# One 129-column product for the high and low values of three query blocks in four, and one bfloat16 product for a tile's sum of squares

## The chip, the cores and the metric

The kernel runs on one core of a Trainium2 chip. The core has a matrix engine (PE, with weight loads listed apart as PEld), three engines for elementwise work (DVE, ACT, POOL), a queue engine (SP) and 16 DMA engines. Each compute engine works through its own instructions in order. The metric is the device time of one execution in microseconds (us); lower is better.

## The reference, cut to what matters

One decoder layer over 2048 tokens of width 1024: a normalised and modulated input, one input projection, two attention branches (A, forgetting attention over all earlier keys; B, sliding window), a gate on each, an output projection, a second normalisation and the residual. The change lies in the value product of branch A and in a scale of the output projection.

```
def forgetting_attention(q, k, v, f_logit):
    cum = jnp.cumsum(jax.nn.log_sigmoid(f_logit), axis=1)
    ...
        s = jnp.einsum('bhqd,bhkd->bhqk', qb, kh) * scale
        s = s + cb[..., None] - cum[:, :, None, :]
        s = jnp.where(causal, s, -jnp.inf)
        p = jax.nn.softmax(s, axis=-1)
        return jnp.einsum('bhqk,bhkd->bhqd', p, vh)
...
y = jnp.concatenate([oa, ob], axis=-1) @ w_out[l]
x = x + gate[:, None, :] * rms_norm(y, g_post[l])
```

Branch A has 8 heads of 64 columns. Inputs and output are float32.

## The kernel before

Products of float32 accuracy are made from 16-bit parts: a value is split into a high part (float16) and a low part (what is left, again in float16), and a product is the sum of high by high, high by low and low by high. For a value block of head `hd` and key block `b` the tile `vt[:, b, hd, :]` holds 129 columns (`VW = 129`): columns 0 to 63 the high part, column 64 ones, columns 65 to 128 the low part. The column of ones gives the sum of the softmax weights in the same product.

The program runs in three stages that overlap at their ends: projections and branch B (until about 420 us), branch A (until about 1000 us), and the output projection (from about 950 us to the end). In all of them the order of the work is written out by hand.

**Branch A.** A head is cut into 4 chunks of 512 queries (`ci` 0 to 3), and a chunk into steps of two key blocks: 2, 4, 6 and 8 steps, 20 for a head and 160 in all. A chunk's four 128-query blocks are numbered `u` 0 to 3. A step goes through these stations:

- `scores` (lines 1341 to 1352): the products into the PSUM tile `sta`;
- `exp32` (1356, ACT): the exponential into `p`, three buffers;
- `high` (1360, ACT) and `low` (1363, DVE): the high and the low part of the weights into `pha`, three buffers;
- `pv` (1365 to 1377, PE), two steps later: for each key block and each query block at or below the diagonal three products, high by high with the ones (65 columns, line 1373), high by low (64 columns, 1375) and low by high with the ones (65 columns, 1376), each with a weight load of its own, all added into columns 0 to 64 of block `u` of the PSUM tile `poa`.

After the last step of a chunk (lines 1378 to 1383) DVE takes the reciprocal of the sums (`a_ri`) and multiplies the four blocks by it in one instruction, out of PSUM into `ona`. `poa` has one buffer. So the first value product of the next chunk (line 1373) waits until DVE has read the last of `poa`.

The main loop issues for each step: its `exp32`, the `low` of the step before, a half of the other work (projections for the next heads, line 351; products for a row maximum, line 1300, whose DVE reductions are lines 1303 and 1305; on DVE also weight maxima, splits and gates), its `high`, the next step's `scores`, the `pv` of two steps before, and the other half. The row-maximum products, projections and small products share five PSUM banks named `bk`.

**Output projection.** For each of the 16 tiles of 128 tokens, `Out.turn` makes the gated input, sums its squares on ACT into one column `gs` (line 1510), adds that column over the 128 partitions with a product of a matrix of ones (line 1514, float32, one column wide), and derives a scale from the bits of the sum (`root_scale`, lines 125 to 129: a rough reciprocal square root by a shift, undone later by `inv`). The tile is split with that scale (1524 and 1525) and multiplied by the output weights (line 1576).

Of the kernel before, what the change touches and what calls it, by code (L numbers as in the profile page):

```python
# [10 lines left out]
F32 = mybir.dt.float32  # L11
F16 = mybir.dt.float16
BF16 = mybir.dt.bfloat16
# [3 lines left out]
ALU = mybir.AluOpType  # L17
AX = mybir.AxisListType

P = 128  # L20
# [4 lines left out]
CH = 512  # L25
# [10 lines left out]
XM, XR, VW = 66, 69, 129  # L36
# [7 lines left out]
def hybrid_layer(  # L44
# [17 lines left out]
    V, A, G, PE, SP = nc.vector, nc.scalar, nc.gpsimd, nc.tensor, nc.sync  # L62
# [20 lines left out]
    def sm(n, tag):  # L83
        return small.tile([P, n], F32, tag=tag, name=tag)
# [40 lines left out]
    def root_scale(dst, ss):  # L125

        h = small.tile([P, 1], I32, tag="rs_h", name="sc_h")
        V.tensor_scalar(h[:], ss.bitcast(I32), 1, None, op0=ALU.logical_shift_right)
        V.tensor_scalar(dst.bitcast(I32), h[:], -1, 0x5F3759DF + (15 << 23), op0=ALU.mult, op1=ALU.add)
# [35 lines left out]
    ones = const.tile([P, P], F32, name="ones")  # L165
# [20 lines left out]
    def bank(hold=False):  # L186
        n = next(n for n in order_ if n not in held)
        order_.remove(n)
        order_.append(n)
        if hold:  # L190
            held.add(n)
        return n
# [9 lines left out]
    def after(n, f):  # L202
        late.append([n, f])
# [79 lines left out]
    def o_store(on, pool, ci, rows_, cols_, eng, lag):  # L283
        if ci == 0:
            eng.dma_start(o_d[0][rows_, cols_].rearrange("(u p) c -> p u c", p=P), on)
            return
        u0, u1 = rows_.start // P, rows_.stop // P
        oh = pool.tile([P, u1 - u0, 2, on.shape[-1]], F16, tag="oh", name="oh")

        def low():  # L290
            V.tensor_tensor(oh[:, :, 1], on, oh[:, :, 0], op=ALU.subtract)
            eng.dma_start(o_d[ci][u0:u1, :, :, cols_].rearrange("u n p c -> p (u n) c"),
                          oh[:].rearrange("p u n c -> p (u n) c"))

        after(lag, lambda: A.activation(oh[:, :, 0], on, AF.Copy))
        after(lag + 1, low)
# [134 lines left out]
    def turn(ci, k, px=None):  # L431

        px = px or ps_x.tile([P, CH], F32, tag="x", name="px")
        for u in range(4):
            PE.transpose(px[:, u * P:(u + 1) * P], xt[ci * 4 + u][:, k * P:(k + 1) * P], ident[:])
        hf = hst.tile([P, CH], F32, tag="hf", name="hf")
        hi, lo = hT[ci][:, 0, k, :], hT[ci][:, 1, k, :]

        def scaled():
            for dst in ([hi] if k % 2 == 0 else []) + [hf[:]]:  # L440
                A.activation(dst, px[:], AF.Identity, scale=Gp[:, k:k + 1], bias=Shp[:, k:k + 1])

        def split():
            if k % 2:
                V.tensor_copy(hi, hf[:])
            V.tensor_tensor(lo, hf[:], hi, op=ALU.subtract)

        return scaled, split

    def turn_x(ci, k):  # L450
        scaled, split = turn(ci, k)
        after(1, scaled)
        after(2, split)
# [9 lines left out]
    start = ExitStack()  # L463
    st = start.enter_context(tc.tile_pool(name="start", bufs=1, reuse_waits="tile"))
    wad = start.enter_context(tc.tile_pool(name="wad", bufs=8, reuse_waits="tile"))
    with tc.manual_schedule():
# [172 lines left out]
        w_low("kb", 0, 1)  # L639
        w_low("vb", 0, 1)  # L640
        turned = [turn(0, k) for k in range(5)]
        squares(1)
        shf0 = col8("shf0")
# [9 lines left out]

        PE.transpose(bk[0][0:1, 0:P], bmx[:], ident[:])
        turned += [turn(0, k, bk[k - 4]) for k in (5, 6)]
        bm = st.tile([1, 1], F32, name="bm")
        V.tensor_reduce(bm[:], bk[0][0:1, 0:P], axis=AX.X, op=ALU.max)
# [215 lines left out]
    class Pair:  # L873
# [65 lines left out]
        def pv(self):  # L939
            j, i = self.j, self.i  # L940
            po = ps_pv.tile([P, 4, 64], F32, tag="pv", name="pob")
            for e, (i_, k0, nk) in enumerate(self.blocks):
                for h in range(2):
                    for b in range(nk):
                        for n, (pp_, vv) in enumerate(((0, 0), (0, 1), (1, 0))):
                            PE.matmul(po[:, 2 * e + h, :], self.ptt[b + 2 - nk][:, pp_, 2 * e + h, :],
                                      vb[:, k0 + b, self.g, 64 * vv:64 * vv + 64],
                                      start=(b == 0 and n == 0), stop=(b == nk - 1 and n == 2))

            def out_():  # L950
                on = onp.tile([P, 2, P], F32, tag="on", name="on")
                V.tensor_tensor(on[:].rearrange("p e (h d) -> p (e h) d", h=2), po[:],
                                self.rinv[:].unsqueeze(2).broadcast_to([P, 4, 64]), op=ALU.mult)
                o_store(on[:], onp, i // 4, slice((i % 4) * P, (i % 4 + 2) * P), slice((4 + j) * P, (5 + j) * P), G, 1)

            after(1, out_)
# [248 lines left out]
    def fox_pool(name, bufs, **kw):  # L1205
        return fox.enter_context(tc.tile_pool(name=name, bufs=bufs, reuse_waits="tile", **kw))

    ps_st = fox_pool("ps_st", 1, space=PSUM)
    ps_po = fox_pool("ps_po", 1, space=PSUM)
# [57 lines left out]
    vt, lk, lq = fx["vt"], fx["lk"], fx["lq"]  # L1267
# [63 lines left out]
    class Step:  # L1331
# [33 lines left out]
        def pv(self):  # L1365
            hd, ph = self.hd, self.ph
            if self.first:
                self.po_[0] = ps_po.tile([P, 4, 65], F32, tag="po", name="poa")
            po = self.po_[0]
            for n, (b, u0, o) in enumerate(self.blocks):  # L1370
                for u in range(u0, 4):
                    pq = slice(o + (u - u0) * P, o + (u - u0 + 1) * P)
                    PE.matmul(po[:, u, :], ph[:, 0, pq], vt[:, b, hd, 0:65],  # L1373
                              start=(self.first and n == 0 and u == 0), stop=False)
                    PE.matmul(po[:, u, 0:64], ph[:, 0, pq], vt[:, b, hd, 65:VW], start=False, stop=False)  # L1375
                    PE.matmul(po[:, u, :], ph[:, 1, pq], vt[:, b, hd, 0:65], start=False,  # L1376
                              stop=(self.last and n == len(self.blocks) - 1))
            if self.last:
                rinv = sm(4, "a_ri")
                V.reciprocal(rinv[:], po[:, :, 64])  # L1380
                on = op_.tile([P, 4, 64], F32, tag="ona", name="ona")
                V.tensor_tensor(on[:], po[:, :, 0:64], rinv[:].unsqueeze(2).broadcast_to([P, 4, 64]), op=ALU.mult)  # L1382
                o_store(on[:], op_, self.ci, slice(0, CH), slice(hd * 64, (hd + 1) * 64), SP, 1 if hd == 7 else 2)

        po_ = {}
# [76 lines left out]
    class Out:  # L1462
# [24 lines left out]
        def turn(self, lag):  # L1487

            if self.t < 4:
                px = [bk[bank()][:].rearrange("p (k n) -> p k n", k=4) for _ in range(2)]  # L1490
                for k in range(KT):
                    PE.transpose(px[k // 4][:, k % 4, :], self.o[:, k * P:(k + 1) * P], ident[:])
            self.hl = wpool.tile([P, 2, KT, P], F16, tag=("whl", "wraw")[self.t % 2], name="oz")
            self.sc = sm(1, "w_pw")
            hi, lo = self.hl[:, 0], self.hl[:, 1]
            gs = sm(1, "w_mx")

            def gate():
                if self.t < 4:
                    for h in range(2):  # L1500
                        z = self.z[:, 4 * h:4 * h + 4, :]
                        V.tensor_tensor(z, px[h], z, op=ALU.mult)
                    return
                of = ozp.tile([P, KT, P], F32, tag="of", name="of")
                V.tensor_tensor(of[:], self.oT[:, 0], self.oT[:, 1], op=ALU.add)
                V.tensor_tensor(self.z, of[:], self.z, op=ALU.mult)  # L1506

            def squares_():
                junk = stp.tile([P, KT, P], BF16, tag="st", name="zj")
                A.activation(junk[:], self.z, AF.Square, accum_out=gs[:])  # L1510

            def scale_():
                pg = bk[bank()][:, 0:1]
                PE.matmul(pg, ones[:], gs[:], start=True, stop=True)  # L1514
                root_scale(self.sc[:], pg)

                self.inv = sm(1, "w_sw")
                V.tensor_tensor(self.inv[:], self.sc[:], ysc[:], op=ALU.mult)
                V.reciprocal(self.inv[:], self.inv[:])

            after(1, gate)
            after(2, squares_)
            after(lag, scale_)
            after(lag + 1, lambda: A.activation(hi, self.z, AF.Copy, scale=self.sc[:]))
            after(lag + 2, lambda: V.scalar_tensor_tensor(lo, self.z, self.sc[:], hi, op0=ALU.mult, op1=ALU.subtract))  # L1525
# [109 lines left out]
    with tc.manual_schedule():  # L1635
# [35 lines left out]
        for s, stp_ in enumerate(steps):  # L1671
            hd, r = divmod(s, NS)
# [111 lines left out]
```

## Time and profile before

| | us |
|---|---|
| time, median of 3 runs | 1157.41 (1156.38 to 1158.7) |
| the profiled execution | 1157.8 |
| its span, from the first to the last instruction | 1156.1 |
| PE busy | 1116.8 (97% of the span) |
| DVE busy | 930.5 (80%) |
| ACT busy | 661.4 (57%) |

The groups of instructions name a line, an engine, an operation, the tiles written and read, a shape and a count, then the busy time in us, the mean of one in ns, and the idle time before them. A matmul's row runs from its start until its results are out, and the next one starts long before that; so how long a stream of products takes is read from the distances of their starts. In the timeline the first number is the start from the beginning of the span, the second how long the instruction, or the merged run of instructions, lasted. A bracket behind a row tells how long the engine was idle before it and what ended that.

### The profile page before, as it was taken

What the parts mean: (1) busy time and instruction counts of PE and PEld (TensorE: products, weight loads), DVE (VectorE), ACT (ScalarE), POOL (GpSimd) and SP (SyncE); (2) the same over time, 40 slices, a digit from 0 to 9 for tenths busy, and PEclk for the clock granted to TensorE, in tenths of its full rate; (3) what the DMA queues carried; (4) which work ended last, traced back from release to release, by engine and by line L of the source; (5) the groups of instructions that cost most, each with busy time, mean ns of one, the idle gap of its engine ahead of it and who ended that gap; (6) DMA issues with size and microseconds to landing.
All of it is one profiled execution on the core that took longest, in us unless ns stands there. A gap on an engine that the chain in (4) does not pass through costs nothing. (4 is left out here: it accounts for less than half of the span.)

```text
span 1156.1 us, 25291 instructions
## 1 busy us (share of the span) xinstructions
PE 1116.8 (97%) x9869; PEld 656.3 (57%) x9869; DVE 930.5 (80%) x2137; ACT 661.4 (57%) x1150; POOL 207.5 (18%) x332
## 2 busy tenths in 40 slices
PE   5899999999999999999999999999999999999997
PEld 2475544577765866555555555555555555544444
DVE  7877468987888568788988899888888887878885
ACT  2876344654555421666757666666776778534332
POOL 1122134554556530010010110001000000000000
PEclk9899999999999999999999999999999999999999
DMA  9943355433243232442344342123311337686743
GB/s 333 336 116 72 87 78 96 97 63 90 52 92 88 58 87 58 73 108 29 80 64 87 84 67 70 38 49 76 45 43 34 91 101 206 140 225 197 199 135 109
DMA packets 123476, 120.10 MB, mean 104 GB/s; under 512 B 64948, under 2 KB 100828, under 8 KB 123356
## 3 DMA queue, kind: packets, MB, share of 16 engines
q1 hardware_dynamic: 112088, 85.69, 27.6%
q0 software_dynamic: 10832, 32.50, 13.5%
q8 instruction: 77, 1.26, 0.6%
q14 instruction: 43, 0.35, 0.1%
q10 hardware_dynamic: 436, 0.28, 0.1%
HBM read 64.75 MB, written 25.18 MB: 78 GB/s over the span
## 5 line engine op out<-in xcount | busy, mean ns | idle before, releaser
L1356 ACT ACTIVATE p<-sta,lift,scl_qk 128x1024 f32<-128x1024 f32 (+2 forms) x160 | 172.0, 1075 | 131.6 <-PE sta L1350 82.6
L351 PE MATMUL bk<-hT,wh_qk 128*128 128x512 f16 x768 | 194.7, 378 | 0.0
L1363 DVE TENSOR_TENSOR pha<-p,pha 128x1024 f16<-128x1024 f32 (+2 forms) x160 | 169.1, 1057 | 0.2 <-ACT pha L1360 0.2
L1303 DVE TENSOR_REDUCE a_m<-bk 128x1 f32<-128x512 f32 x192 | 130.4, 686 | 45.8 <-PE bk L1300 44.8
L1576 PE MATMUL bk<-wohl,oz 128*128 128x512 f16 x744 | 165.3, 379 | 1.1 <-DVE oz L1525 0.7
L1360 ACT ACTIVATE pha<-p 128x1024 f16<-128x1024 f32 (+2 forms) x160 | 148.1, 926 | 5.9 <-PE poa L1376 1.2
L1576 PEld LDWEIGHTS <-oz 128*128 128x128 f16 x744 | 71.9, 99 | 82.8 <-DVE oz L1525 1.8
L1376 PE MATMUL poa<-vt,pha 128*128 128x65 f16 x1088 | 116.1, 192 | 1.4 <-DVE pha L1363 1.2
L1373 PE MATMUL poa<-vt,pha 128*128 128x65 f16 x1088 | 116.6, 193 | 0.8 <-DVE ona L1382 0.7
L1375 PE MATMUL poa<-vt,pha 128*128 128x64 f16 x1088 | 116.6, 194 | 0.0
L351 PEld LDWEIGHTS <-wh_qk 128*128 128x128 f16 x768 | 72.1, 97 | 74.4 <-issue 2.1
L1349 PE MATMUL sta<-T 128*128 128x512 f16 (+1 forms) x320 | 110.9, 346 | 2.8 <-ACT p L1356 2.7
L1300 PE MATMUL bk<-T 66*128 66x512 f16 (+2 forms) x320 | 109.7, 348 | 2.4 <-DVE a_m L1303 1.9
L1373 PEld LDWEIGHTS <-pha 128*128 128x128 f16 x1088 | 101.5, 96 | 15.5 <-DVE ona L1382 1.9
L1350 PE MATMUL sta<-T 69*128 69x512 f16 (+1 forms) x320 | 109.8, 348 | 0.0
L1375 PEld LDWEIGHTS <-pha 128*128 128x128 f16 x1088 | 100.9, 97 | 11.4
L1376 PEld LDWEIGHTS <-pha 128*128 128x128 f16 x1088 | 100.8, 99 | 1.8 <-DVE pha L1363 1.7
L351 PE MATMUL bk<-hT,wh_za 128*128 128x512 f16 x384 | 99.7, 378 | 0.0
L369 PE MATMUL bk<-wh_va,hT 128*128 128x256 f16 x768 | 91.9, 273 | 0.0
L351 PE MATMUL bk<-hT,wh_zb 128*128 128x512 f16 x384 | 91.6, 379 | 0.2 <-DVE qc L754 0.2
L351 PE MATMUL bk<-hT,wh_qb 128*128 128x512 f16 x384 | 91.2, 379 | 0.0
L369 PEld LDWEIGHTS <-hT 128*128 128x128 f16 x768 | 73.3, 98 | 12.2 <-issue 2.1
(459 smaller groups left out, 1919.7 us busy)
## 6 DMA issues: line engine op xcount, KB each, us to landing
hT<-in_x_dram SPq DMA_DIRECT2D x20, 512.0 KB
wa<-in_w_ada_dram SPq DMA_DIRECT2D x16, 512.0 KB
z_d<-tz POOLq DMA_DIRECT2D x32, 256.0 KB, 3.0
T<-z_d SPq DMA_DIRECT2D x16, 512.0 KB
T<-stq SPq DMA_DIRECT2D x62, 128.0 KB
out_dram<-hT SPq DMA_DIRECT2D x15, 512.0 KB
xt<-in_x_dram SPq DMA_DIRECT2D x12, 512.0 KB
qs<-qf SPq DMA_DIRECT2D x80, 64.0 KB
```

What stands on the lines that cost most here:

```text
L351: PE.matmul(ps, whl[:, a, k, :], hT[ci][:, b, k, :], start=(k == 0 and n == 0), stop=(k == KT - 1 and n == 2))
L369: PE.matmul(ps[:, (u % 2) * 2 * P:(u % 2 + 1) * 2 * P], hT[ci][:, a, k, u * P:(u + 1) * P], wv[p][:, b, k, :], start=(k == 0 and n == 0), ...
L1303: V.tensor_reduce(m3[:, u, pc:pc + 1], mx[:, :w], axis=AX.X, op=ALU.max)
L1349: PE.matmul(self.st[:, o:o + w], T[:, 3, kb_], T[:, 1, qc], start=True, stop=False)
L1350: PE.matmul(self.st[:, o:o + w], T[0:XR, 2, kb_], T[0:XR, 0, qc], start=False, stop=not diag)
L1356: A.activation(self.p32[:, :self.w], self.st[:, :self.w], AF.Exp, scale=scl[f"qk{self.hd}"][:], bias=lift[:])
L1360: A.activation(self.ph[:, 0, :self.w], self.p32[:, :self.w], AF.Copy)
L1363: V.tensor_tensor(self.ph[:, 1, :self.w], self.p32[:, :self.w], self.ph[:, 0, :self.w], op=ALU.subtract)
L1373: PE.matmul(po[:, u, :], ph[:, 0, pq], vt[:, b, hd, 0:65], start=(self.first and n == 0 and u == 0), stop=False)
L1375: PE.matmul(po[:, u, 0:64], ph[:, 0, pq], vt[:, b, hd, 65:VW], start=False, stop=False)
L1376: PE.matmul(po[:, u, :], ph[:, 1, pq], vt[:, b, hd, 0:65], start=False, stop=(self.last and n == len(self.blocks) - 1))
L1576: PE.matmul(py, self.hl[:, i, k, :], w_slot(8 * j + k)[:, cc], start=(k == 0 and m_ == 0), stop=(k == KT - 1 and m_ == 2))
```

## The change

Two places are edited. In `Step.pv` the products high by high and high by low become one product of 129 columns for query blocks 0, 1 and 2, whose results lie side by side in PSUM (block `u` begins at column 129 `u`). Four such blocks would be 516 columns, and the tile is one bank of 512; so block 3 keeps the three products and its 65 columns. The normalisation has to add the two halves of blocks 0 to 2. In `Out.turn` the column of sums of squares enters its product as bfloat16, read as the upper 16 bits of each float32, and so does the matrix of ones; the scale that comes of it may differ by a little, and is undone by the same `inv`.

```
-                self.po_[0] = ps_po.tile([P, 4, 65], F32, tag="po", name="poa")
-            po = self.po_[0]
+                self.po_[0] = ps_po.tile([P, CH], F32, tag="po", name="poa")
+            whole = self.po_[0]
+            po = [whole[:, VW * u:VW * u + (VW if u < 3 else 65)] for u in range(4)]
...
-                    PE.matmul(po[:, u, :], ph[:, 0, pq], vt[:, b, hd, 0:65],
+                    PE.matmul(po[u], ph[:, 0, pq], vt[:, b, hd, 0:VW if u < 3 else 65],
                               start=(self.first and n == 0 and u == 0), stop=False)
-                    PE.matmul(po[:, u, 0:64], ph[:, 0, pq], vt[:, b, hd, 65:VW], start=False, stop=False)
-                    PE.matmul(po[:, u, :], ph[:, 1, pq], vt[:, b, hd, 0:65], start=False,
+                    if u == 3:
+                        PE.matmul(po[u][:, 0:64], ph[:, 0, pq], vt[:, b, hd, 65:VW], start=False, stop=False)
+                    PE.matmul(po[u][:, 0:65], ph[:, 1, pq], vt[:, b, hd, 0:65], start=False,
                               stop=(self.last and n == len(self.blocks) - 1))
...
-                V.reciprocal(rinv[:], po[:, :, 64])
+                V.reciprocal(rinv[:], whole[:, 64:3 * VW + 65:VW])
                 on = op_.tile([P, 4, 64], F32, tag="ona", name="ona")
-                V.tensor_tensor(on[:], po[:, :, 0:64], rinv[:].unsqueeze(2).broadcast_to([P, 4, 64]), op=ALU.mult)
+                p3 = whole[:, 0:3 * VW].rearrange("p (u c) -> p u c", u=3)
+                V.tensor_copy(on[:, 0:3], p3[:, :, 65:VW])
+                V.tensor_tensor(on[:, 0:3], p3[:, :, 0:64], on[:, 0:3], op=ALU.add)
+                V.tensor_scalar(on[:, 3], po[3][:, 0:64], rinv[:, 3:4], None, op0=ALU.mult)
+                V.tensor_tensor(on[:, 0:3], on[:, 0:3], rinv[:, 0:3].unsqueeze(2).broadcast_to([P, 3, 64]), op=ALU.mult)
...
             gs = sm(1, "w_mx")
+            gs1 = gs[:].bitcast(BF16)[:, 1:2]
...
-                PE.matmul(pg, ones[:], gs[:], start=True, stop=True)
+                PE.matmul(pg, ones[:].bitcast(BF16).rearrange("p (n two) -> p two n", two=2)[:, 1], gs1,
+                          start=True, stop=True)
```

Of the 1088 triples of value products 768 belong to blocks 0 to 2 (in a head, block `u` meets 4 `ci` + `u` + 1 key blocks in chunk `ci`: 28, 32 and 36 over the four chunks, 96, times 8 heads), and 320 to block 3.

Three places show what the change moves. The first is PE in `pv`, in the first step of the program that has all four query blocks. `pha` are the weights' high and low parts. Before, each query block is:

```order
L1373 LDWEIGHTS pha
L1373 MATMUL poa<-vt,pha 128x65
L1375 LDWEIGHTS pha
L1375 MATMUL poa<-vt,pha 128x64
L1376 LDWEIGHTS pha
L1376 MATMUL poa<-vt,pha 128x65
```

Now, for blocks 2 and 3 (the shapes name the columns of the product):

```order
L1374 LDWEIGHTS pha
L1374 MATMUL poa<-vt,pha 128x129
L1378 LDWEIGHTS pha
L1378 MATMUL poa<-vt,pha 128x65
L1374 LDWEIGHTS pha
L1374 MATMUL poa<-vt,pha 128x65
L1377 LDWEIGHTS pha
L1377 MATMUL poa<-vt,pha 128x64
L1378 LDWEIGHTS pha
L1378 MATMUL poa<-vt,pha 128x65
```

Block 2 has lost a product and its weight load; block 3 stands as before.

The second is DVE at the end of the first head. Before:

```order
L1303 TENSOR_REDUCE a_m<-bk_138 128x1
L1380 RECIPROCAL a_ri<-poa 128x4
L1382 TENSOR_TENSOR ona<-poa,a_ri 128x256
L1303 TENSOR_REDUCE a_m<-bk_6030 128x1
L1363 TENSOR_TENSOR pha<-p_7565,pha 128x384
```

Now:

```order
L1382 RECIPROCAL a_ri<-poa 128x4
L1385 COPY ona<-poa 128x192
L1386 TENSOR_TENSOR ona<-poa,ona 128x192
L1387 TENSOR_SCALAR ona<-poa,a_ri 128x64
L1388 TENSOR_TENSOR ona<-ona,a_ri 128x192
L1303 TENSOR_REDUCE a_m<-bk_6030 128x1
L1363 TENSOR_TENSOR pha<-p_7479,pha 128x384
```

One instruction became four, three of which read `poa`; the reduction and the split behind them keep their order.

The third is PE around the sum of squares in the output projection (`oz` is the split input, `w_mx` the column of sums). Before:

```order
L1576 LDWEIGHTS oz
L1576 MATMUL bk_6030<-wohl,oz 128x512
L1514 MATMUL bk_136<-w_mx,ones 128x1
L1576 LDWEIGHTS oz
L1576 MATMUL bk_6030<-wohl,oz 128x512
```

Now the line has a weight load of its own:

```order
L1521 LDWEIGHTS ones
L1521 MATMUL bk_136<-w_mx,ones 128x1
```

It stands between the same neighbours. The profile of before shows the float32 form of it as two weight loads and two products.

## The prediction

> **What bounds the kernel now.** I read the table of busy times by stretch first, then the waits of PE, then the timeline around the places where PE waits for the normalisation. The stretch of branch A, whole and in five pieces, each bounded by reciprocals of line 1380 (columns: stretch, its length, then busy us and counts of PE, PEld, DVE, ACT, POOL, PE clock, DMA share, GB/s):
>
> ```profile
> 476.49:999.94 523.45, 515.41 (x5397) 301.32 (x5396) 454.25 (x992) 370.61 (x453) 33.89 (x54) 1.00 0.34 76
> 508.82:536.50 27.68, 27.68 (x294) 16.20 (x292) 23.64 (x47) 17.86 (x22) 4.30 (x6) 1.00 0.41 101
> 536.50:544.77 8.27, 8.23 (x71) 4.47 (x69) 8.24 (x15) 6.37 (x9) 1.62 (x3) 1.00 0.06 5
> 672.55:680.44 7.89, 7.89 (x67) 4.22 (x66) 7.74 (x14) 6.94 (x8) 1.64 (x3) 1.00 0.10 14
> 809.93:816.41 6.48, 6.39 (x58) 3.37 (x57) 6.45 (x13) 4.08 (x6) 0.56 (x2) 1.00 0.13 20
> 915.01:938.30 23.29, 20.28 (x252) 12.51 (x251) 23.11 (x43) 19.93 (x27) 0.00 (x0) 1.00 0.27 71
> 938.30:944.21 5.91, 5.91 (x57) 3.27 (x55) 5.42 (x13) 4.46 (x5) 0.00 (x0) 1.00 0.12 20
> ```
>
> PE sets the pace: 515.41 of 523.45 us. But DVE is at 454.25, and its 69 us of idle time lie unevenly. The long last chunk of a head leaves it 4 us (27.68 less 23.64); where a new head begins it has 0.03, 0.15 and 0.03 us, and 0.18 in the 23 us from 915. There DVE is a second bound. The waits of PE in this stretch say the same (in total, times, longest):
>
> ```profile
> PE bk L1300 <- DVE a_m L1303: 1.7, 4, 0.7
> PE poa L1376 <- DVE pha L1363: 1.2, 2, 0.6
> PE poa L1373 <- DVE ona L1382: 0.7, 1, 0.7
> PEld L1373 <- DVE ona L1382: 1.9, 3, 0.9
> ```
>
> So a saving on PE counts nearly everywhere, and added DVE work counts at a few places. Both sides have to be worked out.
>
> **The value products.** Here is the start of the second chunk of the second head. DVE is late, PE waits for `ona`, and then the triples stream:
>
> ```profile
> 544.33 0.22 PE L1352 MATMUL sta<-dmaskT,identb 128*128 128x128 bf16 x1
> ...
> 544.51 0.22 PE L1352 MATMUL sta<-dmaskT,identb 128*128 128x128 bf16 x1
> 544.77 0.17 DVE L1380 RECIPROCAL a_ri<-poa 128x4 f32<-128x4 f32 x1
> 544.98 0.42 DVE L1382 TENSOR_TENSOR ona<-poa,a_ri 128x256 f32<-128x256 f32 x1
> 545.32 0.69 DVE L1305 CUSTOM_DVE_ANT_0 bk<-bk,cmask 128x512 f32<-128x512 f32 x1
> ...
> 545.46 0.20 PE L1373 MATMUL poa<-vt,pha 128*128 128x65 f16 x1 [0.73 <-DVE ona L1382]
> ...
> 545.56 0.19 PE L1373 MATMUL poa<-vt,pha 128*128 128x65 f16 x1
> ...
> 546.02 0.19 PE L1373 MATMUL poa<-vt,pha 128*128 128x65 f16 x1
> ```
>
> From 545.56 to 546.02 are five triples: 92 ns each, 30.7 ns a product. The price of 129 columns lies between these rows (136 columns, a run of 24; 512 columns, a run of 5; the 1-column product follows):
>
> ```profile
> 78.12 1.58 PE L795 MATMUL bk<-wh_vb,hT 128*128 128x136 f16 x24
> ...
> L795 PE MATMUL bk<-wh_vb,hT 128*128 128x136 f16 x384 | 24.6, 223 | 0.2 <-DVE mxs L1010 0.2
> ...
> 1012.54 1.24 PE L1576 MATMUL bk<-wohl,oz 128*128 128x512 f16 x5
> 1013.62 0.28 PE L1514 MATMUL bk<-w_mx,ones 128*128 128x1 f32 x2
> 1013.76 1.02 PE L1576 MATMUL bk<-wohl,oz 128*128 128x512 f16 x4
> ```
>
> A run lasts its starts plus the last one's own time. 136 columns: (1580 - 223) / 23 = 59 ns. 512 columns: starts at 1012.54 and, five later, at 1013.62, so 216 ns. The slope is 157 / 376 = 0.42 ns a column, and 129 columns come to 56 ns. The dearer bound is the 128-column mask products above: three starts between 544.33 and 544.51, 60 ns each, with their changes of operand. Two products removed for one added is 61.4 - 56 = 5.4 ns at best, 1.4 at worst; I take 4.0, since the 136-column run is the nearest in kind. Times 768 is 3.1 us (1.1 to 4.1). About a tenth falls into the stretches above where DVE sets the pace and gains nothing: **-2.8 us**.
>
> The Trainium skill, "TensorE: Matmul & The Clock Gate", section "Back-to-back issue gap", says that in a stream of a weight load and a matmul for each product the spacing is set by both, some 81 ns at 128 columns. By that rule 768 products at 81 ns in place of 61.4 for two would add an estimated 15 us. The trace does not agree: 59 ns at 136 columns, each product with a weight load of its own.
>
> **The sum of squares.** After the five products at 1012.54 the float32 product starts on time at 1013.62, and the next product starts 0.14 us later. One pass in place of two cannot cost less than nothing nor more than this; taking a small product's 31 ns for it, 0.11 us are saved. All 16 would be 1.8 us; 13 stand in the last stage, where products run back to back like these, and the other three stand near waits: **-1.5 us** (0 to -2.2).
>
> **The normalisation.** No row shows the new instructions, but these come near:
>
> ```profile
> L841 DVE COPY cm<-bk x1: 414/414/414, 177.0 to 177.0; 128x256 f32<-128x256 f32 x1
> ...
> L1073 DVE SCALAR_TENSOR_TENSOR stq<-bk,stq 128x512 f16<-128x512 f32 x31 | 21.2, 684 | 6.9 <-ACT stq L1080 6.7
> ...
> L1382 DVE TENSOR_TENSOR ona<-poa,a_ri 128x256 f32<-128x256 f32 x32 | 13.6, 424 | 1.1
> ...
> L291 DVE TENSOR_TENSOR oh<-ona,oh 128x256 f16<-128x256 f32 x24 | 10.0, 418 | 0.0
> ```
>
> From 424 ns at 256 columns and 684 at 512 a column costs 1.02 ns. 192 columns are 64 fewer: the copy 0.35 us, the addition 0.36, the last multiplication 0.35; 64 columns out of PSUM 0.23. In the timeline above the dependent instruction starts 0.04 us after the reciprocal's end, and the independent one behind `ona` 0.08 before its end. Laid out so from the reciprocal's start, before: `ona` ends at 0.63, DVE's next starts at 0.55. After: copy 0.21 to 0.56, addition 0.60 to 0.96, block 3 from 0.88 to 1.11, last multiplication 1.03 to 1.38, next at 1.30. So each of the 32 normalisations holds DVE 0.75 us longer, and `poa` is read 0.48 us later. If nothing overlapped it would be 0.96 and 0.6.
>
> All 32 make 24 us, of which most falls into DVE's idle 69. What does not is found by following the delay to the next place where PE waits for DVE. These rows give the places beside 545.46 (a normalisation's end, and PE's first product behind it):
>
> ```profile
> 578.77 0.42 DVE L1382 TENSOR_TENSOR ona<-poa,a_ri 128x256 f32<-128x256 f32 x1
> ...
> 680.65 0.42 DVE L1382 TENSOR_TENSOR ona<-poa,a_ri 128x256 f32<-128x256 f32 x1
> ...
> 681.13 0.20 PE L1373 MATMUL poa<-vt,pha 128*128 128x65 f16 x1
> ...
> 684.36 0.19 PE L1375 MATMUL poa<-vt,pha 128*128 128x64 f16 x1
> 684.47 0.20 PE L1376 MATMUL poa<-vt,pha 128*128 128x65 f16 x1
> ...
> 816.62 0.42 DVE L1382 TENSOR_TENSOR ona<-poa,a_ri 128x256 f32<-128x256 f32 x1
> ...
> 817.11 0.20 PE L1373 MATMUL poa<-vt,pha 128*128 128x65 f16 x1
> ...
> 742.61 0.42 DVE L1382 TENSOR_TENSOR ona<-poa,a_ri 128x256 f32<-128x256 f32 x1
> ...
> 743.85 0.19 PE L1373 MATMUL poa<-vt,pha 128*128 128x65 f16 x1
> ...
> 944.41 0.42 DVE L1382 TENSOR_TENSOR ona<-poa,a_ri 128x256 f32<-128x256 f32 x1
> ...
> 945.32 0.19 PE L1373 MATMUL poa<-vt,pha 128*128 128x65 f16 x1
> ```
>
> - At 545.46 the normalisation before it (536.50) has made DVE 0.75 late with 0.03 us of idle time to recover, and this one's reads end 0.48 later: 1.2 us.
> - At 579 PE comes as `ona` ends, with DVE recovered before: 0.5.
> - At 681.13: 0.75 - 0.15 + 0.48 = 1.1; then at 684.47, where the low weights were already awaited (0.11 us between two starts instead of 0.03), the rest of the second 0.75: 1.35 together.
> - The start of the sixth head: 0.5 at its first chunk, 1.2 with the second, at 817.11, where PE starts 0.07 after `ona`.
> - From 915 to 938: 0.75 - 0.18 = 0.6 on the low weights that PE waits for, and 0.2 more at 945.32, which has 0.49 us of slack.
>
> At 743.85 the slack is 0.82 us, more than the later release alone, and I take it that this start and those with more hold. The sum is 5.0 us, by the dearer prices 7.2; I take **+5.5 us**. What is late next is DVE's row-maximum reductions, for whose banks PE waits 1.7 us now; they have the idle time of the last chunk ahead of them, so I add nothing, and this is the largest open point.
>
> The profiled execution took 1157.8: 1157.8 - 2.8 - 1.5 + 5.5 = 1159.0. It is 0.4 over the median of the runs, so the forecast for the median is **1158.6 us**, 0.1% up: no change that a measurement of this kernel tells (0.2%, 2.3 us).
>
> **The rivals.**
>
> *Faster: DVE's idle time takes all but the later release of `poa`.* If DVE's order lets late work slide, only 0.48 us at five starts, 2.4, is lost, against 3.9 + 1.8 of gain: 1157.4 - 5.7 + 2.4 = 1154. For it speaks the 69 us of idle time; against it the three stretches with less than 0.2 us of it.
>
> *Slower: the start of a head becomes DVE's.* At the dear prices (0.96 and 0.6) a chunk end costs 1.56 us of slack, so starts like 743.85 with 0.82 lose 0.74 each, for three heads 2.2; and the four waits for banks grow by 0.96 each, 3.8. With 7.2 that is 13.2, less low gains of 2.5: 1157.4 + 10.7 = 1168. It decides from about 0.85 us more for a normalisation. For it speaks that DVE's lateness carries over from one chunk end to the next where chunks are short; against it that ACT and PE start most of DVE's work, whose idle rows lie between.
>
> *Slower: the weight load sets the distance of the 129-column products.* A row of the value products' loads:
>
> ```profile
> L1376 PEld LDWEIGHTS <-pha 128*128 128x128 f16 x1088 | 100.8, 99 | 1.8 <-DVE pha L1363 1.7
> ```
>
> If a product this long no longer lets the next load run ahead, its distance is the load's 99 ns in place of 61.4 for two: 768 make 29 us, and 1157.4 + 29 - 1.5 + 5.5 = 1190. The 136-column run speaks against it. (It is the mechanism of the Trainium skill's rule named above, whose figure would give 1176.)
>
> **How the numbers follow.** Forecast 0.34 (within 0.2% of before, 1155.1 to 1159.7). DVE's head starts, in any size above 0.2%, 0.32; the weight load 0.06; faster 0.28, mostly with the idle time taking the delay. That makes faster 0.28, same 0.34, slower 0.38. Each of these has much of the chance, so the range covers 1153 to 1167, which leaves out the weight load, the far end of the head starts and a full gain on PE; the forecast's own range is 1156 to 1161.
>
> **What would show it.** In the profile after: 129-column products 56 to 60 ns from start to start; the four instructions 1.2 to 1.4 us from the reciprocal to DVE's next; PE's wait for `poa`, named after line 1387, from 1.9 us (the PEld row) to over 4, at 545, 681 and 811 to 817; no second float32 pass at line 1521. I am wrong on the faster side if those waits stay under 3 us, and on the slower if waits for lines 1303 or 1363 grow by more than 2.

## The result: 0.2% slower, and the profile after

| | before | after |
|---|---|---|
| median, range of 20 runs each (us) | 1157.13 (1155.75 to 1158.8) | 1159.32 (1157.59 to 1162.39) |
| the profiled execution, its span | 1157.8, 1156.1 | 1159.25, 1157.5 |

The ratio is 1.0021, with a 95% interval of 1.0013 to 1.0029: 2.4 us more (1.5 to 3.4). The forecast was 1158.6, and called its change too small for a measurement to tell; with 20 runs of each the interval does not hold 1.

The table of busy times of after, over branch A and over the pieces that answer to those shown of before (columns as there: stretch, length, busy us and counts of PE, PEld, DVE, ACT, POOL, PE clock, DMA share, GB/s):

```profile
476.25:1002.31 526.06, 512.85 (x4632) 297.11 (x4631) 472.07 (x1086) 370.74 (x453) 33.88 (x54) 1.00 0.33 75
508.35:535.88 27.53, 27.53 (x252) 16.06 (x250) 24.27 (x50) 17.86 (x22) 4.30 (x6) 1.00 0.40 101
535.88:544.79 8.91, 8.25 (x65) 4.40 (x63) 8.88 (x18) 7.06 (x9) 1.62 (x3) 1.00 0.23 14
672.66:680.98 8.32, 8.32 (x65) 4.50 (x64) 8.29 (x18) 6.91 (x8) 1.64 (x3) 1.00 0.01 1
810.33:817.44 7.11, 6.65 (x54) 3.51 (x53) 7.08 (x16) 4.37 (x7) 0.56 (x2) 1.00 0.15 21
915.72:939.64 23.92, 20.29 (x210) 12.16 (x209) 23.75 (x46) 20.01 (x27) 0.00 (x0) 1.00 0.25 68
```

PE has 2.6 us less to do and is idle 13.2 us instead of 8.0; DVE has 17.8 more. The long chunk (second row) is shorter than before, 27.53 against 27.68. The starts of heads are longer, by 0.64, 0.43 and 0.63 us (8.27, 7.89 and 6.48 before). There DVE had 0.03, 0.15 and 0.03 us of idle time, and now has 0.03 in each: where it is full, the stretch grows by about what DVE was given.

The waits of PE in branch A (in total, times, longest):

```profile
PEld L1374 <- DVE ona L1387: 5.2, 5, 1.9
PE poa L1374 <- DVE ona L1387: 3.7, 5, 1.7
PE poa L1378 <- DVE pha L1363: 2.3, 4, 0.8
PE bk L1300 <- DVE a_m L1303: 1.8, 4, 0.7
```

The wait for the normalisation has grown from 1.9 to 5.2 us in the row of the weight loads, and in that of PE's products from one place with 0.7 us to five with 3.7. The wait for the row maxima, the open point, has not (1.7 before). The first of the five places, in the timeline:

```profile
544.79 0.17 DVE L1382 RECIPROCAL a_ri<-poa 128x4 f32<-128x4 f32 x1
544.88 0.33 DVE L1385 COPY ona<-poa 128x192 f32<-128x192 f32 x1
...
545.24 0.36 DVE L1386 TENSOR_TENSOR ona<-poa,ona 128x192 f32<-128x192 f32 x1
545.52 0.27 DVE L1387 TENSOR_SCALAR ona<-poa,a_ri 128x64 f32<-128x64 f32 x1
...
545.71 0.35 DVE L1388 TENSOR_TENSOR ona<-ona,a_ri 128x192 f32<-128x192 f32 x1
...
545.85 0.23 PE L1374 MATMUL poa<-vt,pha 128*128 128x129 f16 x1 [1.72 <-DVE ona L1387]
...
545.98 0.69 DVE L1305 CUSTOM_DVE_ANT_0 bk<-bk,cmask 128x512 f32<-128x512 f32 x1
...
546.22 0.22 PE L1374 MATMUL poa<-vt,pha 128*128 128x129 f16 x1
...
546.48 0.20 PE L1374 MATMUL poa<-vt,pha 128*128 128x65 f16 x1
...
546.52 0.19 PE L1377 MATMUL poa<-vt,pha 128*128 128x64 f16 x1
```

Three readings. From the reciprocal to DVE's next instruction are 1.19 us, against 0.55 before (544.77 to 545.32): 0.64 more. The last read of `poa` ends at 545.79, 1.00 after the reciprocal's start, against 0.63 before: 0.37 later. And from 546.22 to 546.48 run the pairs of blocks 0, 1 and 2, 87 ns each instead of 92 for a triple.

The sum of squares in the output projection, behind it the next product 0.03 us later instead of 0.14:

```profile
1016.42 0.17 PE L1521 MATMUL bk<-w_mx,ones 128*128 128x1 bf16 x1
1016.45 1.89 PE L1584 MATMUL bk<-wohl,oz 128*128 128x512 f16 x8
```

### The profile page after: what moved, and what is told of

It reads as the page before. It is cut to its first block, busy times and chain, and to the rows that moved or that the text cites. A ratio compares the mean times of both kernels' runs of the same rounds, so it can differ in the third digit from the quotient of the medians.

```text
span 1157.5 us, 23811 instructions
## 1 busy us (share of the span) xinstructions
PE 1113.7 (96%) x9085; PEld 650.4 (56%) x9085; DVE 947.6 (82%) x2233; ACT 661.6 (57%) x1150; POOL 207.9 (18%) x332
## 3 DMA queue, kind: packets, MB, share of 16 engines
q0 software_dynamic: 10832, 32.50, 13.2%
## 5 line engine op out<-in xcount | busy, mean ns | idle before, releaser
L1374 PE MATMUL poa<-vt,pha 128*128 128x129 f16 (+1 forms) x1088 | 113.4, 213 | 3.7 <-DVE ona L1387 3.7
L1378 PE MATMUL poa<-vt,pha 128*128 128x65 f16 x1088 | 113.5, 193 | 2.3 <-DVE pha L1363 2.3
L1374 PEld LDWEIGHTS <-pha 128*128 128x128 f16 x1088 | 98.8, 97 | 18.9 <-DVE ona L1387 5.2
L1378 PEld LDWEIGHTS <-pha 128*128 128x128 f16 x1088 | 96.4, 98 | 14.5 <-DVE pha L1363 3.1
L394 POOL DMA_DIRECT2D z_d<-tz x32 | 17.7, 554 | 294.2 <-DVE tz L392 209.4
L1305 DVE CUSTOM_DVE_ANT_0 bk<-bk,cmask 128x128 f32<-128x128 f32 (+3 forms) x128 | 62.6, 497 | 4.3 <-PE bk L1300 3.9
```

The costliest lines, as they stand in the source:

```text
L1374: PE.matmul(po[u], ph[:, 0, pq], vt[:, b, hd, 0:VW if u < 3 else 65], start=(self.first and n == 0 and u == 0), stop=False)
L1378: PE.matmul(po[u][:, 0:65], ph[:, 1, pq], vt[:, b, hd, 0:65], start=False, stop=(self.last and n == len(self.blocks) - 1))
```

## The experiments

Each run, of 4 to 11 executions, is compared with the kernel before on the same chip. The ratios are to before as it ran there, with medians of 1157.61 us for e1 to e4, 1156.90 for e5 to e8, 1157.44 for e9 to e11 and 1156.98 for e12. Beside the medians, the table gives two stretches of each kernel's profiled execution, read from the row of the reciprocals (first and last start) and the span: branch A from the first to the last reciprocal, and the tail from there to the end. The row of before, and as the second that of after (operation, count, duration min/median/max in ns, first and last start):

```profile
L1380 DVE RECIPROCAL a_ri<-poa x32: 169/176/183, 476.5 to 999.9; 128x4 f32<-128x4 f32 x32
```

```profile
L1382 DVE RECIPROCAL a_ri<-poa x32: 173/177/183, 476.2 to 1002.3; 128x4 f32<-128x4 f32 x32
```

Before: 999.9 - 476.5 = 523.4, and 1156.1 - 999.9 = 156.2. The first reciprocal stands between 475.0 and 477.9 in the fourteen profiles, though no kernel is changed ahead of branch A; so single spans differ by up to 2.9 us for nothing, and the two stretches tell more. Branch A of e1 and e7 is that of before, and their rows agree with it to 0.1 us.

| run | median us | ratio, 95% interval | branch A | tail |
|---|---|---|---|---|
| before | 1157.13 | | 523.4 | 156.2 |
| after | 1159.32 | 1.0021 (1.0013 to 1.0029) | 526.1 | 155.2 |
| e1 bfloat16 sum alone | 1156.36 | 0.9991 (0.9983 to 1.0000) | 523.3 | 154.5 |
| e2 change without it | 1161.66 | 1.0039 (1.0023 to 1.0054) | 526.2 | 156.8 |
| e3 wide products, short normalisation | 1157.79 | 0.9999 (0.9991 to 1.0008) | 523.6 | 156.1 |
| e4 three products, long normalisation | 1165.0 | 1.0060 (1.0048 to 1.0072) | 528.5 | 156.8 |
| e5 as e3, `z` loaded before `o` | 1155.84 | 0.9988 (0.9978 to 0.9999) | 524.2 | 156.2 |
| e6 before, two DVE instructions more | 1166.14 | 1.0073 (1.0061 to 1.0086) | 530.6 | 157.0 |
| e7 as e1, `z` loaded before `o` | 1154.99 | 0.9981 (0.9972 to 0.9990) | 523.3 | 154.6 |
| e8 change, ACT helps | 1179.39 | 1.0192 (1.0178 to 1.0206) | 545.7 | 155.5 |
| e9 as e3, `z` loaded early | 1154.0 | 0.9973 (0.9963 to 0.9983) | 520.7 | 156.1 |
| e10 before, one DVE instruction more | 1160.96 | 1.0032 (1.0020 to 1.0045) | 525.8 | 156.6 |
| e11 wide in chunks 1 and 2 alone | 1155.64 | 0.9986 (0.9977 to 0.9995) | 523.5 | 154.5 |
| e12 as e11, until the seventh head's second chunk | 1154.79 | 0.9981 (0.9972 to 0.9991) | 523.5 | 154.6 |

**The parts one by one (e1 to e4).** e1 is the kernel before with the edit at line 1514 alone; e2 is the change without it. e3 and e4 take the wide products and the normalisation apart. e3 keeps the products and normalises in one instruction, through a view that strides over the blocks, and so leaves the high-by-low part of blocks 0 to 2 out of the output:

```
-                V.tensor_copy(on[:, 0:3], p3[:, :, 65:VW])
...
-                V.tensor_tensor(on[:, 0:3], on[:, 0:3], rinv[:, 0:3].unsqueeze(2).broadcast_to([P, 3, 64]), op=ALU.mult)
+                p4 = bass.AP(whole[:].tensor, whole[:].offset, [whole[:].ap[0], (VW, 4), (1, 64)])
+                V.tensor_tensor(on[:], p4, rinv[:].unsqueeze(2).broadcast_to([P, 4, 64]), op=ALU.mult)
```

e4 keeps the three products, puts the high-by-low one in columns of its own, and has the four instructions:

```
-                    PE.matmul(po[:, u, 0:64], ph[:, 0, pq], vt[:, b, hd, 65:VW], start=False, stop=False)
+                    lo_ = po[u][:, 65:VW] if u < 3 else po[u][:, 0:64]
+                    PE.matmul(lo_, ph[:, 0, pq], vt[:, b, hd, 65:VW], start=False, stop=False)
```

Expected of e1:

> The kernel before with the bfloat16 sum of squares alone. Theory of the prediction: 1.5 us less than before, ratio 0.9987 (1155.6 against 1157.1), with 0.03 us instead of 0.14 from the product's start to the next one in the last stage. Rival (the change's loss comes from this edit, the sum arriving at its wait no sooner): ratio 1.000 or more.

Expected of e2:

> The change without the bfloat16 sum: 129-column products and the four-instruction normalisation. Theory: 1.5 us more than the changed kernel, 1160.8, ratio to before 1.0032. Rival (the bfloat16 edit is what costs): 1157 to 1158, ratio 1.000.

Expected of e3:

> The 129-column products with a normalisation of one instruction, as long as before; it leaves the high by low part of blocks 0 to 2 out of the output (the products that make it run). The float32 sum stands. Theory: the products alone gain 2.8 us, ratio 0.9976 (1154.3). Rival, wide products dear or no shorter: ratio 1.000 or more (29 us more if the load sets the distance).

Expected of e4:

> Three products as before (65, 64 and 65 columns, the high by low part of blocks 0 to 2 into columns of its own) and the four-instruction normalisation; float32 sum. Theory: the normalisation alone costs 5.5 us, ratio 1.0048 (1162.6), with waits of PE for line 1387's kind of instruction over 4 us. Rival, DVE's idle time takes it: 1.0 to 2.4 us, ratio 1.001 to 1.002.

The bfloat16 sum acts in the tail, 156.2 to 154.5, and nowhere else. The long normalisation by itself makes branch A 5.1 us longer and the tail 0.6. With the wide products beside it (e2) branch A is 2.3 shorter than in e4. But with the short normalisation they bring nothing: e3 missed its expectation, and its row and its waits around the hand-over to the output projection tell where the gain went.

```profile
L1382 DVE RECIPROCAL a_ri<-poa x32: 167/174/183, 476.7 to 1000.3; 128x4 f32<-128x4 f32 x32
```

```profile
DVE T L1505 <- DMA T<-z_d: 4.5, 1, 4.5
ACT sv L1513 <- DVE T L1505: 3.3, 1, 3.3
PEld bk L1517 <- ACT sv L1513: 2.6, 1, 2.6
PE bk L1517 <- ACT sv L1513: 2.1, 1, 2.1
```

The timeline of SP's queue in e3 (`o_d` and `z_d` are the attention's output and the gate in memory):

```profile
940.62 0.58 SPq L1436 DMA_DIRECT2D sv<-in_w_out_dram  x1
942.47 0.38 SPq L285 DMA_DIRECT2D o_d<-ona  x1
945.95 0.33 SPq L1482 DMA_DIRECT2D T<-o_d  x1
946.51 0.37 SPq L1488 DMA_DIRECT2D T<-z_d  x1
```

The gate of the first tile (line 1505) waits for `z`, the squares for the gate, and PE's product of the squares for these. The load of `z` stands on SP behind that of `o`, which waits for the store of the last head's first chunk. The same queue in before, and its wait for the squares (total, times, longest):

```profile
944.86 0.38 SPq L285 DMA_DIRECT2D o_d<-ona  x1
946.91 0.33 SPq L1479 DMA_DIRECT2D T<-o_d  x1
```

```profile
PEld bk L1514 <- ACT sv L1510: 0.2, 1, 0.2
```

The store goes out 2.4 us sooner in e3, the load behind it only 1.0, and PE, which came sooner too, waits 2.1.

**The hand-over (e5, e7, e9).** e5 and e7 issue the load of `z` ahead of that of `o`, in e3 and e1. e9 loads `z` of the first two tiles (512 KB each) some 20 us sooner:

```
+            if hd == 7 and r in (1, 2):
+                outs[r - 1].load("z")
             if hd == 7 and r in (4, 6):
-                outs[r // 2 - 2].load()
+                outs[r // 2 - 2].load("o")
```

Expected of e5, e7 and e9 in this order:

> The kernel of the wide products with the one-instruction normalisation (the high-by-low part of query blocks 0 to 2 stays out of the output), and in Out.load the load of the gate z issued ahead of the load of o. Theory: the 2.6 us that its reciprocals were ahead of before until the seventh head are lost at the hand-over to the output projection, where DVE's gate waits for T<-z_d, whose issue stands on SP behind a load that waits for the store of ona; with z first that wait is gone and 1.5 to 2.6 us reach the end: 1155.0 to 1156.2 against 1157.6. Rival 1: the transfers of o, z and the output weights fill the DMA engines there, so the order does not matter and the load of o is as late as z was: 1157.5 to 1158. Rival 2: the gain is lost in the output projection itself: the gate starts earlier, the time stays at 1157.5 to 1158.

> The kernel before with the bfloat16 sum of squares, which took 1.0 to 1.3 us by itself, and the load of z issued ahead of that of o. In before the gate waits for PE's transposes and not for z, so by the theory of the hand-over the order adds nothing here: 1156.1 to 1156.7, as without it. If the order of loads helps whatever comes before (fewer late transfers in the output projection), 1155.5 or less; if o is late now, 1157 or more.

> The wide products with the one-instruction normalisation (the high-by-low part of query blocks 0 to 2 stays out of the output), and the gate z of the first two tiles is loaded in the second and third step of the last head, some 50 us before it is needed, so that 1 MB less stands in the DMA queue at the hand-over. Theory: PE's lead of 2.6 us is lost there to a transfer that is late, because four loads of 512 KB and those of the output weights share the DMA engines; without the two of z the load of o lands in time, the lead stays 1.5 to 2.6 us at the 30th to 32nd reciprocal, and the time is 1155.0 to 1156.0 against 1157.2. Rival 1: it is the store of ona, not the queue, that the load of o waits for: the lead still falls under 0.5 us. Rival 2: the lead stays at the reciprocals and is lost later in the output projection: 1156.8 or more.

The two waits of e5 that took the place of that for `z`; then the reciprocals of e9 and its first load of `z`:

```profile
DVE T L1505 <- PE bk L1495: 4.4, 1, 4.4
...
PE bk L1495 <- DMA T<-o_d: 2.1, 1, 2.1
```

```profile
L1382 DVE RECIPROCAL a_ri<-poa x32: 167/174/183, 475.0 to 995.7; 128x4 f32<-128x4 f32 x32
```

```profile
925.73 0.37 SPq L1491 DMA_DIRECT2D T<-z_d  x1
```

With the order changed (e5), `o` is late instead of `z`: the first rival, in this trace. But the profiled execution took 1158.38 us and is the second slowest of eleven; their median, 1155.84, lies where the theory had it. The intervals of e5 and e3 overlap, so whether the order by itself helps stays open. So it does for e7 against e1: its median lies in the range given for an order that helps whatever comes before, but its two stretches are those of e1 to 0.1 us.

With `z` of two tiles out of the way (e9) PE waits for neither: branch A is 2.7 us shorter than before, all of the wide products' gain reaches the end, and the interval lies wholly below e3's. `z` went out at 925.73, 23 us before the gate of the first tile reads it (948.95) and not some 50, since SP's other loads stand ahead of it.

The starts of the reciprocals show where the gain goes. The 29th stands before the hand-over and the 30th behind it; the lead is that over before, counted from the first reciprocal (us):

| | first | 29th | 30th | lead at the 29th | lead at the 30th |
|---|---|---|---|---|---|
| before | 476.49 | 944.21 | 955.44 | | |
| e7 | 475.45 | 943.13 | 954.36 | 0.0 | 0.0 |
| e3 | 476.70 | 941.81 | 955.53 | 2.6 | 0.1 |
| e5 | 476.26 | 941.36 | 956.46 | 2.6 | -1.3 |
| e9 | 475.02 | 940.12 | 951.29 | 2.6 | 2.7 |
| e12 | 475.22 | 942.00 | 954.39 | 0.9 | -0.2 |
| after | 476.25 | 945.63 | 957.40 | -1.7 | -2.2 |

So e3, e5 and e9 have the same lead from the wide products before the hand-over, and only e9 keeps it. Neither the kernel before with the early `z` alone nor the whole change with it was run; the wait of before there, 0.2 us, leaves it little to gain. The early load does not suffice in every case: e12, below, has it too and loses its lead.

**What the long normalisation costs by (e6, e10).** Both are the kernel before, where `poa` comes free as early as ever; DVE gets one or two instructions more:

```
                 V.tensor_tensor(on[:], po[:, :, 0:64], rinv[:].unsqueeze(2).broadcast_to([P, 4, 64]), op=ALU.mult)
+                V.tensor_tensor(on[:], on[:], on[:], op=ALU.max)
+                V.tensor_tensor(on[:], on[:], on[:], op=ALU.max)
```

> The kernel before with two instructions on DVE behind each normalisation (the maximum of ona with itself, some 0.42 us each, out of and into SBUF): DVE is held about 0.9 us longer, but poa is released as early as before. Theory of the prediction (the delay counts at the starts of heads, the later release counts apart): some 3 to 4 us, 1160.6 to 1161.6 against 1157.6, about half of the 7.4 us that the four-instruction normalisation cost by itself. Rival 1: DVE's idle time takes the delay and only the later release costs: 1157.6 to 1158. Rival 2: the time is all DVE's occupation and the release is nothing: 1164 to 1165.

> The kernel before with one instruction on DVE behind each normalisation, the maximum of ona with itself, 0.42 us; two of them held DVE 0.92 us longer and cost 9.2 us, though poa came free as early as before. If the cost is in proportion to DVE's time, half of it: 4.2 to 5 us, 1161.4 to 1162.2 against 1157.2. If there is idle time to use up first, 1 to 2.5 us, 1158.2 to 1159.7; if the first piece costs most, 6 or more.

The rows of e6:

```profile
L1382 DVE TENSOR_TENSOR ona<-poa,a_ri x32: 423/424/425, 475.9 to 1006.5; 128x256 f32<-128x256 f32 x32
L1383 DVE TENSOR_TENSOR ona<-ona x32: 424/424/426, 476.4 to 1006.9; 128x256 f32<-128x256 f32 x32
L1384 DVE TENSOR_TENSOR ona<-ona x32: 424/425/427, 476.8 to 1007.4; 128x256 f32<-128x256 f32 x32
```

```profile
PEld L1373 <- DVE ona L1382: 4.2, 5, 1.5
...
PE poa L1373 <- DVE ona L1382: 2.8, 3, 1.4
```

Two instructions (some 0.9 us) cost 8.0 us in the two stretches, one (some 0.45) 2.8; the ratios say 8.4 (7.1 to 9.9) and 3.7 (2.3 to 5.2). So the theory of e6, 3 to 4 us, was wrong and its second rival came; e10 came out between its first two cases. PE waits for `ona` longer although its read ends as soon after the reciprocal as before: the reciprocal itself is late, because the normalisation before it held DVE. So DVE's time alone suffices. By the stretches it costs more than in proportion, which the ratios leave open. That idle time takes the first piece is the reading that fits: between the fifth and the sixth reciprocal e10 falls no further behind before, e6 another 0.3 us.

The later release of `poa` shows by itself at one place, the normalisation that begins at 578.56 in before. From there to the next reciprocal are 27.16 us in before, in e6 and in e10, where `poa` comes free as early as ever, but 27.54 in e4. In after PE's first product behind it waits for the last read:

```profile
579.92 0.23 PE L1374 MATMUL poa<-vt,pha 128*128 128x129 f16 x1 [0.25 <-DVE ona L1387]
```

**ACT in DVE's place (e8).** The whole change, with `z` ahead of `o`, and two of the four instructions on ACT:

```
-                V.tensor_copy(on[:, 0:3], p3[:, :, 65:VW])
+                A.activation(on[:, 0:3], p3[:, :, 65:VW], AF.Copy)
+                A.activation(on[:, 3], po[3][:, 0:64], AF.Copy, scale=rinv[:, 3:4])
```

> The whole change, with z loaded ahead of o, and in the normalisation ACT copies the low halves out of PSUM and scales block 3, so that DVE has the reciprocal, the addition and the last multiplication left: some 0.9 us instead of 1.35, against 0.6 before. If DVE's occupation and the release of poa set the cost, the normalisation costs 2 to 3 us instead of 7, and with 2.6 us of gain by the wide products and 1.2 by the bfloat16 sum the time is 1155.5 to 1157. Rival: ACT's copy waits for the last value product in front of the next exponential, and PE waits for p instead (its waits for lines 1356 and 1360 grow by more than 2 us): 1159 or more.

A normalisation in its timeline:

```profile
536.20 0.68 DVE L1303 TENSOR_REDUCE a_m<-bk 128x1 f32<-128x512 f32 x1
...
536.80 0.17 DVE L1382 RECIPROCAL a_ri<-poa 128x4 f32<-128x4 f32 x1
...
537.00 0.33 ACT L1385 ACTIVATE ona<-poa 128x192 f32<-128x192 f32 x1 [3.24 <-DVE a_ri L1382]
537.23 0.31 ACT L1386 ACTIVATE ona<-poa,a_ri 128x64 f32<-128x64 f32 x1
...
537.42 1.21 ACT L1356 ACTIVATE p<-sta,lift,scl_qk 128x1024 f32<-128x1024 f32 x1
...
537.57 0.36 DVE L1387 TENSOR_TENSOR ona<-poa,ona 128x192 f32<-128x192 f32 x1 [0.60 <-ACT ona L1386]
```

The rival came, and worse: 22 us. Between 476 and 1003 us PE waits 23.4 us for the exponential, against 2.7 in before:

```profile
PE sta L1349 <- ACT p L1356: 23.4, 26, 2.2
```

ACT's copy needs nothing that the reciprocal makes, yet it is held until the reciprocal ends, while DVE finishes a reduction first; and the next exponential is queued behind the copy. Of the 3.24 us before the copy 2.2 would have passed anyway, since the last value product that it reads ends at 536.00; the other 1.0 is the wait for DVE. Then DVE waits 0.60 for ACT. The Trainium skill, "PSUM — Partial Sum Buffer", section "PSUM bank collisions raise a hardware error", says that the compiler's scheduler adds a dependency between instructions of two engines on the same bank and the same 32 partitions, reads too. This row agrees: the copy starts 0.03 us after the reciprocal's end. Instead of unloading DVE, the edit tied ACT to DVE's backlog.

**Wide products where DVE has idle time (e11, e12).** Both have the bfloat16 sum and the early `z`, and the long normalisation only in some chunks, with the three products and e3's one-instruction view in the others (here nothing is left out): in e11 in the second and third chunk of each head, in e12 in the same ones, but none after the second chunk of the seventh head.

```
+            wide = self.ci in (1, 2) and 4 * hd + self.ci < 26
...
+                    both = wide and u < 3
+                    PE.matmul(po[u][:, 0:VW if both else 65], ph[:, 0, pq], vt[:, b, hd, 0:VW if both else 65],
```

(The second condition of `wide` is e12's.)

> The change with the wide products, and so the long normalisation, in the second and third chunk of a head alone (384 of the 768 products; their normalisations fall at the start of the third and fourth chunk, 6 and 8 steps long, where DVE has idle time), the three products and the one-instruction normalisation in the first and last chunk; with the bfloat16 sum and the early load of z. Theory: no stall at the starts of heads, half of the gain of the wide products (1.3 to 1.6 us), the bfloat16 sum 1.2 to 1.9: 1153.8 to 1155 against 1157.2, ahead of both kernels. Rival: the long normalisation costs wherever it stands: 16 of 32 of them cost half of 7.4 us: 1157 to 1158.5.

> The wide products in the second and third chunk of heads 0 to 5 and the second of head 6 alone, with the bfloat16 sum and the early load of z. In e11_wide_middle_chunks the reciprocals were 1.1 us ahead at the third chunk of head 6 and 0.5 at the next, since DVE has no idle time between them, and the lead was gone at the end of branch A. Theory: without the long normalisation there the lead of 1.0 us stays to the end, and with 1.2 by the bfloat16 sum and some 0.5 by the early load the ratio is 0.9975 to 0.9980. Rival: in the last head the time is set by something else (loads, ACT), and the lead is lost anyway: 0.9984 to 0.9990, as in e11.

```profile
PEld bk L1507 <- DMA T<-o_d: 1.4, 1, 1.4
PE bk L1507 <- DMA T<-o_d: 0.9, 1, 0.9
```

```profile
942.65 0.36 SPq L285 DMA_DIRECT2D o_d<-ona  x1
946.25 0.33 SPq L1493 DMA_DIRECT2D T<-o_d  x1
```

These are waits of e12 at the hand-over, and its store and load there. e11 lands between its theory and its rival. e12 misses its expectation narrowly by the ratio, but wholly by the mechanism: its lead of 0.9 us does not outlast the hand-over (table above). Branch A is as long as in before, and PE waits 0.9 for `o`, whose load went out 3.6 us after the store that it waits for, against 2.05 in before. Why that store takes 2 us in some profiles and 3.6 in others is not settled. Both kernels are faster than before and after, but with no clear lead over e7, which has no wide products at all. The best version found with the full output is e7 or e12, 0.19% below before (0.09% or 0.10% to 0.28%).

## Why the prediction was right, point by point

- **The sum** was +1.2 us on the profiled execution. The two stretches say +2.7 - 1.0 = +1.7, the ratio +2.4 (1.5 to 3.4), so the forecast change was too small. The forecast lies 0.7 under the measured median, as much as the medians of before differ between the four groups of runs (1156.90 to 1157.61). That it came so near is in part luck: it set out from a median of 1157.41 (three runs), 0.3 over that of twenty.
- **Value products, -2.8.** e9 shows 2.7 in branch A, 3.5 ns for each of the 768 (4.0 taken). In company of the long normalisation (e4 to e2) it is 2.7 at the 29th reciprocal and 2.3 at the end, for the whole change too loses something at the hand-over (0.5 us in the table). The price between the 136-column and the 512-column rows held: with some 30 ns for the 65-column product, a pair's 87 leave 57 for the wide one. So the rival of the weight load falls. The rule of the Trainium skill that I weighed ("TensorE: Matmul & The Clock Gate", section "Back-to-back issue gap", 81 ns at 128 columns) does not hold here.
- **Sum of squares, -1.5.** The tail of e1, e7, e11 and e12 is 1.6 to 1.7 us shorter. The ratio of e1 says 1.0 (0 to 2.0), which does not contradict it.
- **Normalisation, +5.5.** e4 shows 5.1 in branch A and 0.6 in the tail, so 5.7, and 6.9 by its ratio (5.6 to 8.3). The places were right: at the five of the sum (1.2, 0.5, 1.35, 1.2 and 0.8 us) e4's reciprocals fall behind by 1.0, 0.4, 1.1, 1.0 and 0.7; another 0.8 comes behind the 29th reciprocal, where the prediction had nothing. But the size came out in part by luck, since two errors cancel. The four instructions hold DVE 0.64 us longer, not 0.75: I let the copy wait for the reciprocal's end, and it starts 0.08 before it. And I counted the later release of `poa` as 0.48 at five starts, 2.4 of 5. It is 0.37 later; and from e10 (2.8 us for 0.45) and e6 (8.0 for 0.9) I estimate by a straight line some 5 for 0.64 of DVE's time alone, which leaves 0.7 for the release (by the ratios 1.2). So DVE's time weighs well over the 2.6 that I gave it, and the release half of its 2.4 or less. That split is an estimate; only at 579 do the runs show the release apart, as 0.38 us for the 0.5 of the prediction.
- **The rival that only the later release counts (1154)** falls with e6 and e10, where the release is unchanged and the time grows by 8.4 and 3.7 us (ratios). It would hardly have given 1154 in any case: in e3 PE's gain ended at the hand-over. The prediction did not see this wait; in the change itself branch A is late, and it costs some 0.5 us.
- **DVE's head starts at the dear price (1168)** asked for 13.2 us at 0.96 us more for a normalisation; e6 with 0.9, without a later release, costs 8.4 by its ratio. The start at 743.85 costs 0.1 in e6, what 0.9 leaves over its slack of 0.82, and nothing in e4. The waits for banks did not come: that for line 1303 stays at 1.8 us in after, as in the prediction's row (1.7), and is 1.5 in e6. What grows are the waits for `ona` and the low weights.
- **What was to be seen** came: the wait for `poa` at 5.2 us with places at 546, 580, 682 and 811 to 818, no second float32 pass, no growth by 2 us at lines 1303 and 1363. Only the four instructions took 1.19 us, just under the 1.2 to 1.4 named.

## What to carry to other kernels

An engine with 13% of idle time can still set the pace where a stage restarts: look at its idle time stretch by stretch, and price added work by the stretches where it has none. A product that trades PE time for work at the end of a group pays first where the group is long: with the wide products in the middle chunks alone (e11) the 27th reciprocal was 1.1 us ahead of before, where the whole change was 1.0 behind. That lead did not last to the end, so no run here shows it as time gained. Before a gain upstream is counted to the end, look for the first thing downstream that does not move with it, such as a transfer that waits for a store; in e3 it swallowed 2.6 us whole, in e9, with 1 MB loaded earlier, nothing, and in e12, with the same early loads, 1.2.

## What the runs showed of the hardware

The float32 product of one column cost 0.14 us in the stream, its bfloat16 form 0.03. A multiplication of 64 columns out of PSUM by one value for each partition took 0.27 us, that of 256 columns by four 0.42, so a small piece costs much more than its share. An instruction on ACT that shares only a PSUM bank with one on DVE started 0.03 us behind its end, 1.0 us after its own input was complete. Nothing else was unexpected but the store to memory at the hand-over: the load behind it went out 2.0 to 3.6 us after it in the kernels shown.
